# A matmul with batch norm whose instructions a planner orders: the planner's durations replaced by traced ones

## The chip, the cores and the metric

The kernel runs on one core of one Trainium2 chip. The metric is the device time of one execution in microseconds (us), the median of several. The engines are named as in the profile: PE (matrix unit) with PEld (its weight loads), DVE (vector), ACT (scalar), POOL (GpSimd) and SP (which here only issues DMAs).

## The reference

```python
y = np.matmul(x, weight)                      # x 16 x 512 x 1024, weight 1024 x 768, float32
mean = np.mean(y, axis=(0, 1), keepdims=True)
var = np.var(y, axis=(0, 1), keepdims=True)
y_norm = (y - mean) / np.sqrt(var + eps)
return (gamma * y_norm + beta).astype(np.float32)
```

The 16 x 512 rows make 8192. Every output waits for the mean and the variance of its column over all 8192 rows, so no store can start before a column's last product.

## The kernel before

**Tiling.** The rows are 16 chunks `c` of 512 rows (2 MB of x each); the 768 columns are six tiles `nt` of 128. x is loaded as bfloat16 by DMAs that POOL issues (L403, four for a chunk), and turned by DVE transposes (L435, two for a chunk of 512 rows, L428 in chunks 2, 3 and 6) so that the contraction lies on the partitions. Chunk `c` starts at row `m0` = 512 c; below, "the turn of m0=6144" is that of chunk 12.

**Stage 1 (to about 108 us).** While x arrives, column tiles 0 and 1 are computed with rows on the partitions (`rows_unit`, matmuls of L510, two halves of a chunk, 16 matmuls each). Each half is followed by four tasks: ACT squares it into one of three buffers `sq_sb` (L659), DVE adds it to `sum1` (`add_rows`, L662), POOL or DVE adds the squares to `sum2` or `sum3` (`add_squares`, L666), and ACT keeps it as bfloat16 (L672). The gaps of stage 1 are filled with matmuls of column tiles 2 to 5 (L575), ACT copies of some turned chunks (`part_chunk`, L547) and matmuls of L814. Then POOL merges the sums (L795, L800), PE adds them over the partitions (`sums_rows`, L871), and scale and shift follow.

**Stage 2 (to 187 us).** The other column tiles run from the kept x (L575), each followed by statistics (L711) and a copy to bfloat16 (L715, L720). Beside this, finished column tiles are scaled and shifted, brought back to rows by PE transposes (L1044), by DMA transposes (L1106, L1220) or not at all, and stored by DMAs that SP issues (L946, L1085, L1182, L1202).

**Tail (from 187 us).** After the last matmul of column tile 5 (L753) come its statistics, scale and shift, 64 transposes (L1044), ACT copies (L1361) and the last stores (L1364), 4 MB. Two stores of 256 KB held back from column tile 4 (L1255) go ahead of them.

**The planner.** Nothing of this order is written out by hand. Each piece of work is a `Task` with a priority, the engines that can do it, for each of these a pair (time that it occupies the engine, time to its end), and its dependencies and buffers. `arrange` (L122) builds the order when the kernel is built: it takes the engine that can begin something first, among that engine's tasks that can begin within `LOOK` = 0.2 of that moment the one of best priority, and books it. `SEM` is the time between an end and the start that waits for it. `Wires` (L98) books DMAs: one set of wires, serially, with a lead ahead and a tail behind, and eight DMAs under way for a queue. A DVE task with `lock` is not begun while a POOL task is booked, and the other way round. A task with two engines (`add_squares`: POOL or DVE) goes to the one that can begin it first. What `arrange` returns is the order in which each engine executes its instructions; on the chip they then wait for semaphores, and the booked times mean nothing there.

Of the kernel before, what the change touches and what calls it, by code (L numbers as in the profile page):

```python
# [9 lines left out]
class Task:  # L10
# [3 lines left out]
    def __init__(self, prio, engines, emit, deps=(), dma=None, uses=(), takes=()):  # L14
        self.prio, self.engines, self.emit, self.deps = prio, engines, emit, list(deps)
        self.dma, self.uses, self.takes = dma, list(uses), list(takes)
        self.end = self.after = None
        self.hosts = 0
        self.count = 1
        self.lock = False  # L20
        self.slack = self.look = 0.0
        for slot in self.uses + self.takes:
            slot.users.append(self)
# [74 lines left out]
class Wires:  # L98
# [4 lines left out]
    def __init__(self):  # L103
        self.free = 4.3
        self.lanes = {"SP": [], "POOL": [], "ACT": []}
# [16 lines left out]
def arrange(tasks, turns, log=None):  # L122
# [45 lines left out]
    while left:  # L168
# [46 lines left out]
        if t.dma:  # L215
            free[e], t.end = wires.send(e, start, occ, t.dma, t.count)
        t.start, t.engine = start, e
# [10 lines left out]
def kernel(  # L228
# [133 lines left out]
    def dve(occ):  # L362
        return {"DVE": (occ, occ + 0.09)}
# [10 lines left out]
    LINE, PER_KB = 0.00119, 1 / 385.0  # L374
    STORE, XBAR = 1 / 350.0, 1.25

# [71 lines left out]
    for kind, n, *n1 in order:  # L448
# [12 lines left out]
        if m0 == M // 2:  # L461
# [11 lines left out]
        for i in range(rows // QR):  # L473
            c, q = divmod(m0 // QR + i, QPC)
            for j0, j1 in ((0, JW // 2), (JW // 2, JW)) if m0 < CH else ((0, JW),):
                new = q == 0 and j0 == 0
                x_ready[c, q, j1] = task(
                    -1000 + t, dve((2.2 if c in SINGLE else 1.16) * (j1 - j0) / JW + 0.02),
                    turn_x(slot, x_slot[c], m0, i * QR // 32, j0, j1, new), [load],
                    uses=[slot] if new else [slot, x_slot[c]], takes=[x_slot[c]] if new else [])  # L480
                if not new:
                    x_ready[c, q, j1].deps.append(x_ready[c, 0, JW // 2 if m0 < CH else JW])
            x_ready.setdefault((c, q, JW // 2), x_ready[c, q, JW])
        if rows % QR:
            t0 = rows // QR * QR // 32
            m1 = m0 + 32 * t0
            c, q = divmod(m1 // QR, QPC)
            x_ready["tile", m1 // P] = task(
                -1000 + t, dve(0.63), turn_x(slot, x_slot[c], m0, t0, 0, JW, False, P),
                [load, x_ready[c, 0, JW]], uses=[slot, x_slot[c]])  # L490
            x_ready[c, q, JW] = x_ready[c, q, JW // 2] = x_ready["tile", m1 // P]
# [157 lines left out]
    def rows_stats(c, ts, slot, t):  # L649
# [18 lines left out]
        def keep(eng):  # L668
            if "y" not in y_row[c].__dict__:
# [135 lines left out]
    def ga_unit(nt, c, q, cols=QR):  # L805
# [17 lines left out]
        def keep(eng):  # L823
            if "y" not in y_row[c].__dict__:
# [6 lines left out]
        late = 40 if c == C - 1 else -3.0  # L831
        b = task(clock[0] - late, dve(0.609 * cols / CH + 0.05), bn, [t], uses=[slot])
        mine = [h[1] for k, h in ga_half.items() if k[1] == c]
        k = task(clock[0] + 3.4, act(0.48 * cols / CH + 0.03), keep, [b] + mine,
                 uses=[slot] + ([y_row[c]] if mine else []), takes=[] if mine else [y_row[c]])
# [15 lines left out]
    for c in range(RC, C):  # L851
        for q in range(QPC):
            for nt in range(GA):
                ga_unit(nt, c, q)
    merges.append(task(U, dve(0.36), merge(0), [k[1] for k in ends], True))
    merges.append(task(U, pool(0.65), merge(1), [k[2] for k in ends]))
    for h in range(2):
        merges.append(task(U, pool(0.65), more(h), merges[1:]))

# [57 lines left out]
    U = S - 30.0  # L917
    s1 = task(U, pe(0.9), sums_rows, merges, takes=[tot_slot])
    se = task(U, dve(0.8), sums_entry, [s1], True, uses=[tot_slot])
    ag = [task(U, dve(0.25), aggregate_rows(a), [se] + [h[0] for k, h in ga_half.items() if k[0] == a]) for a in range(GA)]  # L920
    rt = task(U, {"ACT": (0.2, 0.3)}, root_rows, ag)
    sc = task(U, dve(0.3), scale_rows, [rt], True)
    sr = task(U + 0.1, dve(0.35), shift_rows, [sc], True)
    p0 = task(U, pe(0.45), spread_rows(0), [sc], takes=[a0_slot])
    p1 = task(U, pe(0.45), spread_rows(1), [sr], takes=[a1_slot])
    p1.look = 0.6
    sh = task(U, act(0.3), shift_sbuf, [p1], uses=[a1_slot])


    def rows_out(c, s0, s1, k):  # L930
# [13 lines left out]
        def store(eng):  # L944
# [4 lines left out]
        keeps = [row_end[k][3] for k in row_end if k[0] == c]  # L949
        a = task(due, dve(0.3 * n), norm, [p0] + keeps, takes=[slot], uses=[y_row[c], a0_slot])  # L950
        b = task(due + 0.4, dve(0.3 * n) if k in ADDED else pool(0.59 * n), add, [a, p1 if k in ADDED else sh],
                 uses=[slot, a1_slot] if k in ADDED else [slot])
        task(due + 1.0, {"SP": (0.38, 0.4)}, store, [b], dma=n * NA * P * 4 / 1024 / 365.0 * 1.024,
             uses=[slot])
# [13 lines left out]
    def finish_tasks(nt):  # L968
# [41 lines left out]
        if nt in ASTAT:  # L1010
            deps = [task(now + 1.0, {"ACT": (1.2, 1.3)}, total, deps)]
        a = task(now + 1.0, dve(0.5), var, deps)
        b = task(now + 1.0, {"ACT": (0.2, 0.3)}, root, [a])
        if nt > GA:
            return task(now + 1.0, dve(0.55), affine, [b], True)
        d = task(now + 1.0, dve(0.1), invert, [b])
# [39 lines left out]
    def ga_block(c, due):  # L1056
# [31 lines left out]
        norms = [task(due, dve(0.25), norm_ga(a), [sr] + [h[1] for k, h in ga_half.items() if k[1] == c], True, uses=[yslot])  # L1088
                 for a in range(GA)]
# [3 lines left out]
        d = task(due, act(0.905), copy, [t], takes=[slot], uses=[bank])  # L1093
        task(due, {"SP": (0.38, 0.4)}, store, [d], dma=RT * NA * P * 4 / 1024 / 365.0 * 1.024, uses=[slot])

# [3 lines left out]
    def raw_turn(nt, c, due):  # L1099
# [3 lines left out]
        def xbar(eng):  # L1103
# [3 lines left out]
            if not gated:  # L1107
# [7 lines left out]

        b = task(due, {"SP": (1.4, 1.4)}, xbar, [col_end[nt, c + i][1] for i in range(GY)] + [gate], dma=XBAR,
                 takes=[slot], uses=[yslot])
        raw[nt, c] = slot, b

# [7 lines left out]
    def raw_spread(nt, fin_task):  # L1127
# [31 lines left out]

        d = task(now, dve(0.35), turn, [fin_task], True)  # L1160
        g = task(now, {"POOL": (0.8, 0.85), "ACT": (0.9, 1.0)}, gather, [d])
        s = task(now, {"POOL": (1.2, 1.25), "ACT": (1.0, 1.1)}, deal, [g])
        t = task(now, act(0.4), keep, [s], takes=[bank])
        raw_aff[nt] = bank, t, s, row[:, 1]

    def raw_block(nt, c, due):
# [17 lines left out]

        a = task(due, dve(1.18), norm_raw, [t, turned], takes=[slot], uses=[bank, rslot])
        on = RAWADD[nt]
# [4 lines left out]
    def col_block(nt, c, due, fin_task, held=False):  # L1191
# [30 lines left out]
        b = task(due + 0.5, {"SP": (1.4, 1.4)}, xbar, [a], dma=XBAR,  # L1222
                 takes=[t_slot] + ([slot] if MODE[nt][c // GY] == "xact" else []), uses=[yslot])
        if MODE[nt][c // GY] == "xpool":
            def store_x(eng):
# [3 lines left out]
        else:  # L1229
# [3 lines left out]

            d = task(due + 1.0, act(0.9), convert, [b], uses=[slot, t_slot])
            d.slack = 1.0
# [32 lines left out]
    for nt in range(GA, NT - 1):  # L1268
        if nt == NT - 2:
            for i, c in enumerate(LATE):  # L1270
                part_chunk(c, clock[0] + 0.0 + 4.0 * i, {"DVE": (0.63, 0.7), "ACT": (1.05, 1.1)},
                           i == 0, 4.0 / 4, [col_end[NT - 3, late[-1]][1]])
# [52 lines left out]

    su = task(E - 5.0, dve(0.5), sum_up, [col_end[nt, c][0] for c in range(C - 2)])
    ag = task(E - 50.0, dve(0.25), aggregate,
# [11 lines left out]
    for c, r0, rows in ends:  # L1339
# [23 lines left out]
        def store(eng, slot=slot, m0=m0, count=count):  # L1363
# [48 lines left out]
```

## Time and profile before

| what | value |
|---|---|
| time, median of 3 runs (lowest, highest) | 205.97 us (205.72, 206.15) |
| profiled execution, first to last instruction (span) | 204.1 us |
| median less span: what lies around the span, if the profiled execution took as long as the median | 1.87 us |
| busy: PE, DVE, ACT, POOL | 189.3, 159.3, 146.2, 124.1 us |
| first matmul of the product, end of the last one | 12.14, 186.6 us |
| HBM read, written | 36.71, 25.17 MB |

The profile keeps one execution. It shows when each instruction began and how long it took, the idle time of an engine and what ended it, and the DMAs; the trace also has the moments at which a DMA's semaphore tells of its landing. A profile of such a kernel is read from PE outwards: first where PE stands still, then how late the data of each of its blocks were ready.

### The profile page before, as it was taken

What the parts mean: (1) busy time and instruction counts of PE and PEld (TensorE: products, weight loads), DVE (VectorE), ACT (ScalarE), POOL (GpSimd) and SP (SyncE); (2) the same over time, 40 slices, a digit from 0 to 9 for tenths busy, and PEclk for the clock granted to TensorE, in tenths of its full rate; (3) what the DMA queues carried; (4) which work ended last, traced back from release to release, by engine and by line L of the source; (5) the groups of instructions that cost most, each with busy time, mean ns of one, the idle gap of its engine ahead of it and who ended that gap; (6) DMA issues with size and microseconds to landing.
All of it is one profiled execution on the core that took longest, in us unless ns stands there. A gap on an engine that the chain in (4) does not pass through costs nothing.

```text
span 204.1 us, 3510 instructions
## 1 busy us (share of the span) xinstructions
PE 189.3 (93%) x1210; PEld 114.5 (56%) x1210; DVE 159.3 (78%) x250; ACT 146.2 (72%) x260; POOL 124.1 (61%) x150
## 2 busy tenths in 40 slices
PE   7969999999999999999999999999999999997900
PEld 3457554657488888777865444444444445544600
DVE  4031879999999999969989998987999878657900
ACT  2001461368989999899978766999998959956950
POOL 7776954877499989997403999389613312940000
PEclk9999999999999999999999999999999999999965
DMA  4999999999999999999686899899999999999998
GB/s 71 172 199 196 176 196 196 196 197 197 190 193 197 197 196 196 196 197 195 103 181 200 297 339 336 248 301 328 295 322 227 336 303 274 347 343 310 310 347 253
DMA packets 98562, 48.74 MB, mean 239 GB/s; under 512 B 24304, under 2 KB 98032, under 8 KB 98544
## 3 DMA queue, kind: packets, MB, share of 16 engines
q0 software_dynamic: 34624, 18.36, 65.5%
q1 hardware_dynamic: 63920, 30.16, 52.6%
q8 instruction: 9, 0.15, 0.3%
q14 instruction: 9, 0.07, 0.1%
HBM read 36.71 MB, written 25.17 MB: 303 GB/s over the span
## 4 chain that ended last, share of the span: by engine, by line
PE 86%; ACT 3%; DMA 3%; POOL 2%; issue 1%; ACTq 0%; DVE 0%; POOLq 0%
PE y_ps L575 54%; PE y_ps L510 24%; PE y_ps L814 4%; ACT o_sb L1361 3%; DMA ring<-in_x_dram 3%; PE o_ps L1044 1%; POOL ring L403 1%; POOL w_sb L387 1%; PE y_ps L753 1%; PE a_ps L903 1%; PE o_ps L1074 0%; ACTq L1407 0%; PE idle_ps L591 0%; PE tot_ps L871 0%; ACT ring L1252 0%
## 5 line engine op out<-in xcount | busy, mean ns | idle before, releaser
L575 PEld LDWEIGHTS <-w_sb 128*128 128x128 bf16 x520 | 50.3, 97 | 57.6
L575 PE MATMUL y_ps<-xT_sb,w_sb 128*128 128x512 bf16 (+1 forms) x272 | 59.3, 371 | 0.0
L575 PE MATMUL y_ps<-x_pl,w_sb 128*128 128x512 bf16 x248 | 57.4, 379 | 0.0
L403 POOL DMA_DIRECT2D ring<-in_x_dram x76 | 47.2, 626 | 14.4 <-DMA ring<-in_x_dram 5.5
L510 PE MATMUL y_ps<-w_sb,xT_sb 128*128 128x256 bf16 x448 | 50.6, 273 | 1.7 <-DMA ring<-in_x_dram 1.6
L510 PEld LDWEIGHTS <-xT_sb 128*128 128x128 bf16 x448 | 43.5, 98 | 9.4 <-DVE xT_sb L435 2.9
L435 DVE STREAM_TRANSPOSE xT_sb<-ring 128x1024 f32<-128x1024 f32 (+1 forms) x29 | 31.2, 1111 | 14.1 <-DMA ring<-in_x_dram 13.9
L711 DVE BATCH_NORM_STATS2 stats<-y_ps 128x6 f32<-128x512 f32 x46 | 30.9, 687 | 7.7 <-PE y_ps L575 7.2
L715 ACT CAST y_sb<-y_ps 128x512 bf16<-128x512 f32 x51 | 29.0, 593 | 10.4 <-DVE stats L711 6.3
L547 ACT COPY x_pl<-xT_sb 128x1024 bf16<-128x1024 bf16 x32 | 32.8, 1063 | 1.7 <-DVE xT_sb L435 1.7
L942 POOL TENSOR_TENSOR ring<-ring,sum 128x1024 f32<-128x1024 f32 (+1 forms) x11 | 23.8, 2188 | 14.9 <-ACT y_ps L724 10.9
L659 ACT ACTIVATE sq_sb<-y_ps 128x512 f32<-128x512 f32 x28 | 16.3, 610 | 16.2 <-PE y_ps L510 15.9
L666 POOL TENSOR_TENSOR sum<-sum,sq_sb 128x512 f32<-128x512 f32 x20 | 25.6, 1278 | 3.0 <-ACT sq_sb L659 1.7
L662 DVE TENSOR_TENSOR sum<-y_ps,sum 128x512 f32<-128x512 f32 x28 | 18.9, 675 | 6.3 <-ACT sq_sb L659 5.3
L672 ACT CAST y_sb<-y_ps 128x512 bf16<-128x512 f32 x28 | 16.3, 594 | 8.2 <-DVE sum L662 8.0
L1178 POOL TENSOR_TENSOR ring<-ring,sum 128x1024 f32<-128x1024 f32 x6 | 14.8, 2477 | 9.8 <-issue 8.5
L937 DVE TENSOR_TENSOR ring<-y_sb,a_ps 128x1024 f32<-128x1024 bf16 (+1 forms) x16 | 16.7, 1079 | 0.1
L1044 PE MATMUL o_ps<-ident,y_sb 128*128 128x128 bf16 x104 | 13.1, 221 | 1.6 <-DVE y_sb L1348 1.5
L1232 ACT CAST ring<-ring 128x1024 f32<-128x1024 bf16 x13 | 13.8, 1063 | 0.6 <-DMA ring<-y_sb 0.6
L1145 POOL COPY sum<-sum 32x256 f32<-32x256 f32 (+1 forms) x17 | 5.8, 340 | 13.4 <-DVE sum L1142 6.5
L428 DVE STREAM_TRANSPOSE xT_sb<-ring 128x2048 bf16<-128x2048 bf16 x6 | 13.5, 2290 | 0.1
L591 PE MATMUL idle_ps<-idle_sb 128*128 128x512 f32 x18 | 9.6, 688 | 1.5 <-DVE idle_sb L316 1.5
(104 smaller groups left out, 153.7 us busy)
## 6 DMA issues: line engine op xcount, KB each, us to landing
out_dram<-ring SPq DMA_DIRECT2D x37, 512.0 KB, 3.4
ring<-in_x_dram POOLq DMA_DIRECT2D x52, 256.0 KB, 8.8
out_dram<-o_sb SPq DMA_DIRECT2D x6, 512.0 KB, 4.7
ring<-in_x_dram POOLq DMA_DIRECT2D x16, 128.0 KB, 5.9
w_sb<-in_weight_dram POOLq DMA_DIRECT2D x8, 192.0 KB, 6.2
out_dram<-ring SPq DMA_DIRECT2D x6, 256.0 KB, 3.0
ring<-in_x_dram POOLq DMA_DIRECT2D x4, 192.0 KB, 7.8
out_dram<-o_sb SPq DMA_DIRECT2D x3, 256.0 KB, 2.5
```

The costliest lines, as they stand in the source:

```text
L403: bi = seq(nc.gpsimd.dma_start(x_bf[32 * i:32 * i + 32], src[:, :, KQ * i:KQ * (i + 1)]))
L435: seq(nc.vector.transpose(dst, src[:, :, jw0:jw1]))
L510: seq(nc.tensor.matmul(y_ps[:, s], x_of(c, jw, e, t * P, (t + 1) * P), w_sb[:, jw, e, 0:NA], start=(s == 0 and jw == 0 and e == 0), stop=( ...
L547: seq(nc.scalar.copy(dst, pairs) if eng == "ACT" else ENG[eng].tensor_copy(dst, pairs))
L575: seq(nc.tensor.matmul(y_ps, w_sb[:, jw, e, nt * P:(nt + 1) * P], moving(c, jw, e, q0 * QR, q1 * QR, parted), start=(jw == 0 and e == 0 an ...
L659: seq(nc.scalar.activation(sq_sb[:, 0:n], slot.tile[:, 0:n], AF.Square))
L662: seq(nc.vector.tensor_add(sum1, slot.tile[:, 0:n], sum1))
L666: seq(ENG[eng].tensor_add(acc, acc, state["sq"][:, 0:n]))
L711: seq(nc.vector.bn_stats(dst, slot.tile))
L715: seq(nc.scalar.copy(y(nt, c), slot.tile))
L937: seq(nc.vector.tensor_mul(slot.o, y_row[c].y[:, s0:s1], aff[0][:, None, :].to_broadcast([P, n, NA])))
L942: seq(ENG[eng].tensor_add(slot.o, slot.o, row[:, None, :].to_broadcast([P, n, NA])))
```

## The change

Only what `arrange` reckons with is changed. No task, dependency, buffer or priority is added or taken away, and no instruction is changed; the order in which the engines execute them follows from the new numbers. The numbers of the lines rise by 1 behind L21, by 7 in all behind L113, by 8 behind L1117 and by 9 behind L1223.

```diff
-        self.free = 4.3
+        self.free = 4.21
-    def send(self, queue, t, hold, took, count):
-        soft = queue == "POOL"
+    def send(self, queue, t, hold, took, count, turned=False):
+        if turned:
+            t = max(t, self.ready(queue))
+            self.free = max(self.free, t + 0.722) + took
+            land = max(self.free + 0.375, t + hold + 1.4)
+            self.lanes[queue].append(land)
+            return max(t + hold, land - 2.325), land
+        first, last = (1.095, 1.0425) if queue == "POOL" else (0.722, 0.441)
         for _ in range(count):
             t = max(t, self.ready(queue)) + hold / count
-            self.free = max(self.free, t + (1.0 if soft else 0.5)) + took / count
-            land = self.free + (1.3 if soft else 0.6)
+            self.free = max(self.free, t + first) + took / count
+            land = self.free + last
...
-    SEM, LOOK = 0.06, 0.2
+    SEM, LOOK = 0.03, 0.2
...
-    STORE, XBAR = 1 / 350.0, 1.25
+    STORE, XBAR, TURN = 1 / 345.85, 1.12, {"SP": (1.143, 1.143)}
...
-            t, {"POOL": (2.68 * rows / CH + 0.535 * also, 2.68 * rows / CH + 0.535 * also)}, load_x(m0, rows, slot, between),
+            t, {"POOL": (2.57 * rows / CH + 0.6 * also,) * 2}, load_x(m0, rows, slot, between),
...
-                    -1000 + t, dve((2.2 if c in SINGLE else 1.16) * (j1 - j0) / JW + 0.02),
+                    -1000 + t, dve((2.2 if c in SINGLE else 1.15) * (j1 - j0) / JW + 0.01),
...
-        s = task((now + 4.2 if c < RC - 2 else 0), {"POOL": (1.36, 1.36 + 0.05), "DVE": (0.62, 0.7)}, add_squares, [a],
+        s = task((now + 4.2 if c < RC - 2 else 0), {"POOL": (1.22, 1.276), "DVE": (0.60, 0.682)}, add_squares, [a],
...
-            part_chunk(c, clock[0] + (4.0 if c < EARLY else 20.0), act(1.05))
+            part_chunk(c, clock[0] + (4.0 if c < EARLY else 20.0), {"ACT": (0.946, 1.056)})
...
-    merges.append(task(U, dve(0.36), merge(0), [k[1] for k in ends], True))
-    merges.append(task(U, pool(0.65), merge(1), [k[2] for k in ends]))
+    merges.append(task(U, {"DVE": (0.489, 0.567)}, merge(0), [k[1] for k in ends], True))
+    merges.append(task(U, {"POOL": (0.70, 0.737)}, merge(1), [k[2] for k in ends]))
...
-        b = task(due + 0.5, {"SP": (1.4, 1.4)}, xbar, [a], dma=XBAR,
+        b = task(due + 0.5, TURN, xbar, [a], dma=XBAR,
+        b.turned = True
...
-        task(due + 0.6 * (n - 1), {"SP": (0.6, 0.6)}, store, [d], dma=count * P * P * 4 / 1024 * STORE * 1.024,
+        task(due + 0.6 * (n - 1), {"SP": (0.4, 0.4)}, store, [d], dma=count * P * P * 4 / 1024 * STORE * 1.024,
```

Some twenty more pairs are changed in the same way by 0.01 to 0.4 us (statistics of the two last chunks, scale and shift, the stores of column tiles 0 and 1, the spreading of a column's scale over rows). `add_rows` keeps its 0.608, L711 its 0.609, L659 its 0.494.

More of the change, by code (lines that the diff above doesn't have):

```diff
@@ L215, in arrange @@
         if t.dma:
-            free[e], t.end = wires.send(e, start, occ, t.dma, t.count)
+            free[e], t.end = wires.send(e, start, occ, t.dma, t.count, t.turned)
         t.start, t.engine = start, e
@@ L831, in ga_unit @@
         late = 40 if c == C - 1 else -3.0
-        b = task(clock[0] - late, dve(0.609 * cols / CH + 0.05), bn, [t], uses=[slot])
+        b = task(clock[0] - late, {"DVE": (0.342, 0.42)}, bn, [t], uses=[slot])
         mine = [h[1] for k, h in ga_half.items() if k[1] == c]
-        k = task(clock[0] + 3.4, act(0.48 * cols / CH + 0.03), keep, [b] + mine,
+        k = task(clock[0] + 3.4, {"ACT": (0.29, 0.375)}, keep, [b] + mine,
                  uses=[slot] + ([y_row[c]] if mine else []), takes=[] if mine else [y_row[c]])
@@ L917 @@
     U = S - 30.0
-    s1 = task(U, pe(0.9), sums_rows, merges, takes=[tot_slot])
-    se = task(U, dve(0.8), sums_entry, [s1], True, uses=[tot_slot])
-    ag = [task(U, dve(0.25), aggregate_rows(a), [se] + [h[0] for k, h in ga_half.items() if k[0] == a]) for a in range(GA)]
+    s1 = task(U, pe(0.81), sums_rows, merges, takes=[tot_slot])
+    se = task(U, {"DVE": (0.63, 0.707)}, sums_entry, [s1], True, uses=[tot_slot])
+    ag = [task(U, {"DVE": (0.25, 0.28)}, aggregate_rows(a), [se] + [h[0] for k, h in ga_half.items() if k[0] == a]) for a in range(GA)]
     rt = task(U, {"ACT": (0.2, 0.3)}, root_rows, ag)
[L922 to L925, printed above, removed]
+    sc = task(U, {"DVE": (0.27, 0.361)}, scale_rows, [rt], True)
+    sr = task(U + 0.1, {"DVE": (0.27, 0.357)}, shift_rows, [sc], True)
+    p0 = task(U, pe(0.48), spread_rows(0), [sc], takes=[a0_slot])
+    p1 = task(U, pe(0.48), spread_rows(1), [sr], takes=[a1_slot])
     p1.look = 0.6
-    sh = task(U, act(0.3), shift_sbuf, [p1], uses=[a1_slot])
+    sh = task(U, {"ACT": (0.28, 0.37)}, shift_sbuf, [p1], uses=[a1_slot])
     def rows_out(c, s0, s1, k):
@@ L1010, in finish_tasks @@
         if nt in ASTAT:
-            deps = [task(now + 1.0, {"ACT": (1.2, 1.3)}, total, deps)]
+            deps = [task(now + 1.0, {"ACT": (0.82, 0.91)}, total, deps)]
         a = task(now + 1.0, dve(0.5), var, deps)
@@ L1014, in finish_tasks @@
         if nt > GA:
-            return task(now + 1.0, dve(0.55), affine, [b], True)
+            return task(now + 1.0, {"DVE": (0.78, 0.87)}, affine, [b], True)
         d = task(now + 1.0, dve(0.1), invert, [b])
@@ L1114, in xbar @@
             seq(bi)
[L1116 removed]
+        b = task(due, TURN, xbar, [col_end[nt, c + i][1] for i in range(GY)] + [gate], dma=XBAR,
                  takes=[slot], uses=[yslot])
+        b.turned = True
         raw[nt, c] = slot, b
@@ L1158, in keep @@
             seq(nc.scalar.copy(a_ps[:, 0:2 * P], row.rearrange("p i n -> p (i n)")))
[L1160 to L1163, printed above, removed]
+        d = task(now, {"DVE": (0.467, 0.543)}, turn, [fin_task], True)
+        g = task(now, {"POOL": (0.98, 1.036), "ACT": (0.91, 1.02)}, gather, [d])
+        s = task(now, {"POOL": (1.43, 1.48), "ACT": (1.15, 1.25)}, deal, [g])
+        t = task(now, {"ACT": (0.302, 0.38)}, keep, [s], takes=[bank])
         raw_aff[nt] = bank, t, s, row[:, 1]
@@ L1183, in store @@
                 out_flat[m0:m0 + n * P, nt * P:(nt + 1) * P].rearrange("(s p) n -> p s n", p=P), slot.o))
-        a = task(due, dve(1.18), norm_raw, [t, turned], takes=[slot], uses=[bank, rslot])
+        a = task(due, {"DVE": (1.13, 1.218)}, norm_raw, [t, turned], takes=[slot], uses=[bank, rslot])
         on = RAWADD[nt]
@@ L1270 @@
             for i, c in enumerate(LATE):
-                part_chunk(c, clock[0] + 0.0 + 4.0 * i, {"DVE": (0.63, 0.7), "ACT": (1.05, 1.1)},
+                part_chunk(c, clock[0] + 0.0 + 4.0 * i, {"DVE": (0.58, 0.67), "ACT": (0.946, 1.056)},
                            i == 0, 4.0 / 4, [col_end[NT - 3, late[-1]][1]])
@@ L1324, in affine @@
         seq(nc.vector.scalar_tensor_tensor(fss, coef, rstd, base, op0=ALU.mult, op1=ALU.add))
-    su = task(E - 5.0, dve(0.5), sum_up, [col_end[nt, c][0] for c in range(C - 2)])
+    su = task(E - 5.0, {"DVE": (0.72, 0.808)}, sum_up, [col_end[nt, c][0] for c in range(C - 2)])
     ag = task(E - 50.0, dve(0.25), aggregate,
```

18 lines of the change are left out of this document (10 added, 8 removed).

## The prediction

> **What bounds the kernel now.** I read the page first, then the windows, the chain of waits, the time lines of DVE and POOL about 80 us, and SP's at the end. The page and the windows:
>
> ```profile
> PE 189.3 (93%) x1210; PEld 114.5 (56%) x1210; DVE 159.3 (78%) x250; ACT 146.2 (72%) x260; POOL 124.1 (61%) x150
> ...
> PE 86%; ACT 3%; DMA 3%; POOL 2%; issue 1%; ACTq 0%; DVE 0%; POOLq 0%
> ...
> 72.00:97.00 25.00, 25.00 (x204) 19.60 (x202) 22.55 (x28) 24.07 (x38) 22.44 (x28) 1.00 1.45 196
> 97.00:108.00 11.00, 11.00 (x94) 8.72 (x93) 9.86 (x28) 9.18 (x28) 2.45 (x6) 1.00 0.76 151
> ```
>
> The first pair of the windows' columns is the length and PE's busy time: from its first product at 12.14 to the last at 186.6 PE stands still for some 0.15 us in all, at clock 1.00. So nothing in the middle can be won. The time is the head (12.14), PE's fixed work (174.5) and the tail (17.5); a new order adds whatever PE is made to wait, and changes the tail.
>
> The tail, from SP's time line (start, length, line, operation, count):
>
> ```profile
> 183.56 1.41 SPq L1182 DMA_DIRECT2D out_dram<-ring  x1
> 187.53 1.20 SPq L1255 DMA_DIRECT2D out_dram<-ring  x2
> 189.31 10.56 SPq L1364 DMA_DIRECT2D out_dram<-o_sb  x11
> ```
>
> By the trace's landing events the store of 183.56 lands at 189.53, and from there the landings follow each other by 0.76 us for 256 KB and 1.51 for 512 KB up to 203.15: the DMAs are the bound of the tail, with a little work still queued when it begins. A store on idle DMAs lands 2.78 after its issue (120.58 to 123.36), that is 1.27 and its 1.51; 1.40 by a 256 KB one (109.10 to 111.25). With nothing queued at 187.5 the two held stores and the four small ones behind them would land at 189.55, 190.31, 190.97, 191.44, 192.32 and 193.08 instead of 190.29 to 193.33. An order that empties the queue is worth 0.25 us (0.13 by the other lead), and no more: **0.2**. Likewise a tail that begins later hides only these 0.2.
>
> **What the change moves.** I compared the built instructions of both kernels, engine by engine. PE's order is the same, except that 32 transposes of L1044 stand four matmuls later at about 170 us, the same number behind the same line: 0. The head's order is the same: 0. On DVE, ACT, POOL and SP tasks change places from 24 us on. Each costs nothing unless PE gets its data or its bank later than it asks for them, so I looked for the blocks of PE with least to spare: those of the last chunks in stage 1, whose turn waits for loads that the DMAs bring at 196 GB/s without a pause (the last column of the windows).
>
> DVE's time line there:
>
> ```profile
> 75.62 2.25 DVE L662 TENSOR_TENSOR sum<-y_ps,sum 128x512 f32<-128x512 f32 x3
> 77.78 0.90 DVE L666 TENSOR_TENSOR sum<-sum,sq_sb 128x512 f32<-128x512 f32 x1
> 78.87 2.37 DVE L435 STREAM_TRANSPOSE xT_sb<-ring 128x1024 f32<-128x1024 f32 x2 [0.20 <-DMA ring<-in_x_dram]
> 81.17 2.25 DVE L662 TENSOR_TENSOR sum<-y_ps,sum 128x512 f32<-128x512 f32 x3
> 83.33 0.68 DVE L666 TENSOR_TENSOR sum<-sum,sq_sb 128x512 f32<-128x512 f32 x1
> 84.02 2.37 DVE L435 STREAM_TRANSPOSE xT_sb<-ring 128x1024 f32<-128x1024 f32 x2
> 86.32 1.45 DVE L662 TENSOR_TENSOR sum<-y_ps,sum 128x512 f32<-128x512 f32 x2
> 89.37 2.37 DVE L435 STREAM_TRANSPOSE xT_sb<-ring 128x1024 f32<-128x1024 f32 x2 [1.60 <-DMA ring<-in_x_dram]
> 91.66 1.02 DVE L666 TENSOR_TENSOR sum<-sum,sq_sb 128x512 f32<-128x512 f32 x1
> ```
>
> The pairs of L435 turn chunks 11, 12 and 13. The first half of chunk 12's pair ends at 85.26 (84.02 and 1.24), and PE takes it at 85.41: 0.15 to spare. Chunk 13 has 0.45 (90.61, 91.06), `sums_rows` 0.1 (99.33, 99.43). Chunks 9 and 10 have 2 or more.
>
> And POOL's:
>
> ```profile
> 68.08 3.84 POOL L403 DMA_DIRECT2D ring<-in_x_dram  x6
> ...
> 74.13 4.00 POOL L666 TENSOR_TENSOR sum<-sum,sq_sb 128x512 f32<-128x512 f32 x3
> 78.06 2.56 POOL L403 DMA_DIRECT2D ring<-in_x_dram  x4
> 80.64 2.64 POOL L666 TENSOR_TENSOR sum<-sum,sq_sb 128x512 f32<-128x512 f32 x2
> 83.22 2.57 POOL L403 DMA_DIRECT2D ring<-in_x_dram  x4
> ```
>
> **Two L666 at once exclude each other.** The DVE one of 77.78 lasts 0.90 and that of 91.66 lasts 1.02, where one alone lasts 0.68. POOL's end at 78.13 (74.13 and 4.00) and 92.13 (90.84 and 1.29); both DVE ones end 0.55 after that. L662, which reads one operand from PSUM, is not held up by them (three in 2.25 at 81.17, as at 75.62, with POOL in L666 from 82.00). The planner knows this rule (`lock`), and keeps them apart by its bookings; on the chip whichever comes first wins. So the question is how well the new numbers place them. The change sets POOL's L666 to 1.22 from 1.36. In the trace three of them take 3.93 to the next instruction (74.13 to 78.06) and two 2.58, so 1.3 each; and `add_rows` is booked at 0.608, where three in a row take 2.25.
>
> The order between chunk 11's turn and chunk 12's, before: DVE L662 three times, L666; after: L662 twice, L666, L662, L666. On POOL, from the load issues of 68.08 on, before: eight L403, three L666, four L403, two L666; after: four L403, two L666, four L403, three L666, four L403, one L666.
>
> POOL after: 68.08 and 2.56 for four issues: 70.64; two L666, 2.58: 73.22; four issues, 2.58: 75.80; three L666, 3.93: 79.73; four issues: 82.31; so its next L666 runs from **82.31 to 83.59**. The loads don't suffer: the issues that move by 2.6 us have 9 and more us to their landing.
>
> DVE after: chunk 11's turn waits for its load as before, and ends at 81.24; two L662, 1.45 from 81.17: 82.62; the next begins 0.08 earlier, as L666 does at 83.33, so at **82.54**. POOL has had the memory since 82.31. DVE's L666 then ends at 83.59 and 0.55: 84.14. L662 from 84.06, the second L666 from 84.66 (0.60 apart, 83.33 less 82.72), the turn from 85.26, its first half ends 1.24 later at 86.50, and PE begins 0.03 behind it: 86.53, where it began at 85.41. **PE waits 1.12.** The Trainium skill (SBUF — State Buffer, section "SBUF: two separate sides") calls this an exclusive lock, in which the later one fully blocks; by that the L666 would take its whole 0.68 behind POOL, and the wait be 1.25. The rows' 0.55 decides.
>
> The other places: a pair collides in the same way at 72.5 ahead of chunk 10's turn; that moves by 0.3, and PE has 2 to spare: 0. Ahead of chunk 13's turn one more L666 of DVE waits for a square (L659) of chunk 12. PE comes to chunk 13 1.12 later itself, at 92.18, and the 0.68 fit in unless the square is over 1 us later than now: 0, at most 0.3. `sums_rows` needs the last L666, merged by L795 and L800 on POOL; all of it follows PE by the same amount: 0, at most 0.2. From 108 to 186 us, PE's banks are free 2 us and more before it asks, the x copies (L547) 5 us; moves of 1 to 2 us there cost 0, at most 0.3. The tail: PE ends 1.12 later, past the queue's end; what was queued no longer matters, which is the 0.2.
>
> **The sum.** 204.1 + 1.12 - 0.2 = 205.0 for the span. The median lies 1.87 above the span of the profiled execution: **206.9 us**, 0.45% more.
>
> **The rivals.** Measurements of this kernel tell about 0.2% (0.4 us) from no change.
>
> 1. *DVE comes first at the port.* It decides at 0.23 us: were POOL's L666 that much later, or DVE's that much earlier, DVE would hold it. For: the 0.23 is what is left of six additions. Against: no row has POOL slower than 1.36 in a row. Price: DVE's L666 from 82.54, L662 83.14, L666 83.74, turn 84.34, half done 85.58; PE waits 0.2. At chunk 13 its L666 goes ahead of the turn, 0.6 against 0.45 and these 0.2; with POOL now late and ACT behind it, 0 to 0.4. In sum 0.2 to 0.6, less 0.2: 206.0 to 206.4, not slower by what can be told.
> 2. *The change does nothing to the time*: the new places find enough room everywhere, and the tail's queue is empty sooner. For: PE now stands still nowhere, with 0.15 here and 0.1 there to spare. Against: the L666 more ahead of chunk 12's turn. 0 to -0.25: 205.7 to 206.0.
> 3. *More than one stall*: the bounds above at once, or a DMA queue that is longer at the tail because POOL's adds (L1178, now three in a row) come later. 0.8 more at most: 207.3 to 207.8.
>
> **The numbers.** Forecast (206.6 to 207.3) 0.60; rival 1 0.22, of it 0.04 over 0.2%; rival 2 0.11, of it 0.05 under -0.2% by what the runs scatter; rival 3 0.07. Slower 0.60 + 0.07 + 0.04 = 0.71; faster 0.05; same 0.24. The range from 205.9 to 207.5 leaves out most of rival 2 and half of rival 3, and holds the low bound of the wait.
>
> **What would show it.** In the profile after, L666 on DVE near 82.5 with 1.5 us instead of 0.68, beside an L666 of POOL; the turn of chunk 12 at 85.2; a wait of PE (L510) for DVE's L435 of about 1.1 in the list of waits, which has none now; PE's last product at 187.7. If that L666 lasts 0.68 and POOL's is the longer one, rival 1 holds; if PE waits nowhere, rival 2. The forecast is wrong if PE waits elsewhere for 0.5 us or more, or if the last stores don't follow PE's end.

## The result, and the profile after

The changed kernel takes **207.25 us** (median of 6 runs, 207.06 to 207.67), the kernel before 206.06 (6 runs as well): ratio 1.0066, 95% interval 1.005 to 1.0081. The ratio is not the quotient of these two medians, which is 1.0058 (1.19 us). The profiled execution took 207.51, its span 205.7 (before 204.1).

In the changed kernel the line numbers are higher by 7 (L435 is L442, L662 is L669, L666 is L673, L659 is L666, L672 is L679, L814 is L821, L871 is L878) or by 8 and 9 in the late part.

The page after; its second line is the shares of the chain of work that ended last:

```profile
PE 190.2 (92%) x1196; PEld 114.7 (56%) x1210; DVE 159.8 (78%) x251; ACT 145.1 (71%) x262; POOL 122.9 (60%) x147
...
PE 44%; DMA 20%; ACT 15%; DVE 7%; issue 5%; POOL 4%; ACTq 1%; DVEq 0%; POOLq 0%
```

No engine has much more work than before: PE's 0.9 us lie ahead of its first product (busy 9.90 us to 12.14, before 9.07). But the chain, of which PE had 86%, now leaves PE and goes through DMA, ACT and DVE: PE is made to wait. Its list of waits (us in total, times, longest) has, beside the wait for the first load, which was there before, two rows in stage 1 that are new:

```profile
PE y_ps L517 <- DMA ring<-in_x_dram: 0.9, 1, 0.9
PE y_ps L517 <- DVE xT_sb L442: 0.5, 2, 0.3
PE y_ps L821 <- ACT y_sb L679: 0.2, 1, 0.2
```

Of the 0.5 us for L442, 0.3 lie at 26 us and only 0.2 at chunk 12. At chunk 14 two things end nearly together: the first half of the turn at 97.93, and at 97.97 ACT's copy L679, which the row names. These waits sum to less than the loss, since a wait is only shown where it stands out between two instructions. A better measure is how much later PE begins the same block. PE's order is nearly the same (4 of its 1210 weight loads differ, in e1, e2, e3 and e7 8 to 28), so each weight load can be laid beside its twin in the trace of before. The table does this at six places, for the profiled execution of every kernel of this study (us later than before), with the length of the tail (from the issue of the first held store, L1255, to the landing of the last store: 15.62 before) and the ratio of the times with its interval.

| kernel | first product, 12.11 | chunk 11, 80.17 | chunk 12, 85.41 | chunk 13, 91.06 | chunk 14, 96.71 | L575 at 173.52 | tail | ratio |
|---|---|---|---|---|---|---|---|---|
| after | 0.12 | 0.27 | 0.71 | 1.02 | 1.36 | 1.69 | 15.61 | 1.0066 (1.005, 1.0081) |
| e4 one add later | -0.12 | 0.08 | 0.44 | 2.77 | 3.12 | 3.45 | 15.61 | 1.0172 (1.014, 1.0205) |
| e6 POOL's add later | 0.22 | 0.39 | 0.48 | 1.15 | 1.16 | 1.15 | 15.62 | 1.0023 (1.0011, 1.0035) |
| e9 ACT's sums later | -0.13 | -0.02 | 0.43 | 0.74 | 0.74 | 0.74 | 15.60 | 1.0045 (1.0029, 1.006) |
| e10 all moves | -0.06 | -0.07 | 0.02 | 0.02 | 1.99 | 1.98 | 15.61 | 1.0170 (1.0134, 1.0206) |
| e11 e6 and e9 | -0.24 | -0.07 | 0.16 | 0.52 | 0.52 | 0.52 | 15.61 | 1.0038 (1.0025, 1.0051) |
| e15 three places | -0.04 | -0.07 | 0.16 | 0.16 | 0.49 | 0.50 | 15.59 | 1.0025 (1.0011, 1.004) |
| e16 e4, four buffers | 0.83 | 0.80 | 1.27 | 2.07 | 2.42 | 2.81 | 18.17 | 1.0210 (1.0192, 1.0229) |
| e17 e10, four buffers | 0.24 | -0.05 | 0.04 | 0.04 | 0.04 | 0.10 | 18.16 | 1.0159 (1.0137, 1.018) |
| e1 stage 1 numbers | 1.23 | 1.55 | 2.50 | 2.50 | 2.70 | 3.92 | 17.83 | 1.0235 (1.021, 1.026) |
| e2 other numbers | -0.02 | 0.38 | 0.47 | 0.47 | 0.47 | 0.41 | 16.42 | 1.0049 (1.002, 1.0079) |
| e3 SEM 0.06 | 0.28 | 0.44 | 0.44 | 0.44 | 1.27 | 1.20 | 16.28 | 1.0115 (1.0085, 1.0145) |
| e7 spacing | 0.41 | 0.10 | 0.28 | 0.75 | 1.00 | 2.64 | 15.70 | 1.0104 (1.0087, 1.0122) |

Two rows need a note. In e1 four products stand ahead of transposes at 173.52, so its value there is taken at the last product. In e7 two products stand ahead of the blocks of chunks 11 and 12, so its entries there compare unlike matmuls; what shows at chunk 13 is lost at chunk 12.

The first column differs although the order is the same in all of them to 20 us: it is the scatter of one execution, and the second column holds it too. The ten kernels of the table that have the order of after to 80 us stand between -0.07 and 1.55 there. In the row of after, 0.27 is there by chunk 11; **1.42 more come between 80 and 173 us**, all of them by 100: 0.44 at chunk 12, 0.31 at chunk 13, 0.34 at chunk 14, 0.24 where `sums_rows` (L878) begins and 0.09 within it. The tail is as long as before. The measured 0.66% is 1.36 us. So the loss is made in 20 us at the end of stage 1.

DVE's time line there (start, length, line, count):

```profile
82.54 0.68 DVE L673 TENSOR_TENSOR sum<-sum,sq_sb 128x512 f32<-128x512 f32 x1
83.14 0.68 DVE L669 TENSOR_TENSOR sum<-y_ps,sum 128x512 f32<-128x512 f32 x1
83.74 1.16 DVE L673 TENSOR_TENSOR sum<-sum,sq_sb 128x512 f32<-128x512 f32 x1
84.82 2.35 DVE L442 STREAM_TRANSPOSE xT_sb<-ring 128x1024 f32<-128x1024 f32 x2
...
90.17 0.69 DVE L673 TENSOR_TENSOR sum<-sum,sq_sb 128x512 f32<-128x512 f32 x1 [1.62 <-ACT sq_sb L666]
90.78 2.36 DVE L442 STREAM_TRANSPOSE xT_sb<-ring 128x1024 f32<-128x1024 f32 x2
...
95.48 0.69 DVE L673 TENSOR_TENSOR sum<-sum,sq_sb 128x512 f32<-128x512 f32 x1 [0.97 <-ACT sq_sb L666]
...
96.69 2.36 DVE L442 STREAM_TRANSPOSE xT_sb<-ring 128x1024 f32<-128x1024 f32 x2
```

The three pairs of L442 turn chunks 12, 13 and 14; ahead of each stands an addition of squares. They begin at 84.82, 90.78 and 96.69, where before they began at 84.02, 89.37 and 95.20. The additions ahead of chunks 13 and 14 wait for ACT's squares, and DVE's queue waits with them. POOL's line beside the first:

```profile
79.96 2.57 POOL L410 DMA_DIRECT2D ring<-in_x_dram  x4
82.54 1.80 POOL L673 TENSOR_TENSOR sum<-sum,sq_sb 128x512 f32<-128x512 f32 x1
```

POOL's L673 lasts 1.80, where one alone lasts 1.29. Both began at 82.54; DVE's took its usual 0.68, so DVE came first. At 83.74 the next one of DVE found POOL at it until 84.34, and ended 0.56 behind that. The planner had booked POOL's from 81.29 to 82.51 and DVE's from 82.51: in its plan they don't touch, on the chip POOL is 1.25 late.

ACT's line, with the squares of chunks 12 and 13 (L666):

```profile
89.39 0.74 ACT L666 ACTIVATE sq_sb<-y_ps 128x512 f32<-128x512 f32 x1
90.95 0.60 ACT L666 ACTIVATE sq_sb<-y_ps 128x512 f32<-128x512 f32 x1 [0.82 <-DVE sum L673]
...
94.28 0.60 ACT L727 ACTIVATE y_sb<-y_ps 128x512 bf16<-128x512 f32 x1
...
94.86 0.59 ACT L666 ACTIVATE sq_sb<-y_ps 128x512 f32<-128x512 f32 x1
...
96.28 0.62 ACT L731 ACTIVATE y_ps<-y_ps 128x512 f32<-128x512 f32 x1
...
96.88 0.62 ACT L666 ACTIVATE sq_sb<-y_ps 128x512 f32<-128x512 f32 x1
```

The second square waits for DVE's addition of the first: in the program as it is built, both use the same one of the three buffers. L727 and L731 are the two sums of column tile 2 that stand ahead of the squares of chunk 13.

### The profile page after: what moved, and what is told of

Its sections match the earlier page's. It is cut to its first block, busy times and chain, and to the rows that moved or that the text cites. A ratio compares the mean times of both kernels' runs of the same rounds, so it can differ in the third digit from the quotient of the medians.

```text
span 205.7 us, 3500 instructions
## 1 busy us (share of the span) xinstructions
PE 190.2 (92%) x1196; PEld 114.7 (56%) x1210; DVE 159.8 (78%) x251; ACT 145.1 (71%) x262; POOL 122.9 (60%) x147
## 4 chain that ended last, share of the span: by engine, by line
PE 44%; DMA 20%; ACT 15%; DVE 7%; issue 5%; POOL 4%; ACTq 1%; DVEq 0%; POOLq 0%
PE y_ps L582 34%; DMA ring<-in_x_dram 12%; DMA w_sb<-in_weight_dram 6%; ACT x_pl L554 4%; PE y_ps L821 4%; ACT o_sb L1370 3%; POOL ring L410 3%; ACT sq_sb L666 3%; PE y_ps L517 3%; ACT y_sb L679 2%; DMA ring<-y_sb 2%; PE o_ps L1051 2%; DVE xT_sb L442 1%; DVE x_pl L554 1%; DVE xT_sb L435 1%
## 5 line engine op out<-in xcount | busy, mean ns | idle before, releaser
L582 PE MATMUL y_ps<-xT_sb,w_sb 128*128 128x512 bf16 (+1 forms) x264 | 58.6, 371 | 0.4
L582 PE MATMUL y_ps<-x_pl,w_sb 128*128 128x512 bf16 x242 | 56.6, 379 | 0.3
L442 DVE STREAM_TRANSPOSE xT_sb<-ring 128x1024 f32<-128x1024 f32 (+1 forms) x29 | 31.1, 1109 | 12.6 <-DMA ring<-in_x_dram 12.6
L722 ACT CAST y_sb<-y_ps 128x512 bf16<-128x512 f32 x51 | 28.8, 587 | 13.6 <-DVE stats L718 6.1
L554 ACT COPY x_pl<-xT_sb 128x1024 bf16<-128x1024 bf16 x31 | 31.8, 1069 | 1.7 <-DVE xT_sb L442 1.7
L666 ACT ACTIVATE sq_sb<-y_ps 128x512 f32<-128x512 f32 x28 | 17.0, 626 | 19.0 <-PE y_ps L517 17.2
L673 POOL TENSOR_TENSOR sum<-sum,sq_sb 128x512 f32<-128x512 f32 x20 | 26.1, 1303 | 4.4 <-ACT sq_sb L666 3.8
L1186 POOL TENSOR_TENSOR ring<-ring,sum 128x1024 f32<-128x1024 f32 x6 | 14.3, 2412 | 17.1 <-DVE ring L1182 17.1
L669 DVE TENSOR_TENSOR sum<-y_ps,sum 128x512 f32<-128x512 f32 x28 | 18.9, 674 | 5.9 <-ACT sq_sb L666 4.7
L679 ACT CAST y_sb<-y_ps 128x512 bf16<-128x512 f32 x28 | 15.9, 618 | 2.5 <-DVE sum L669 2.5
L435 DVE STREAM_TRANSPOSE xT_sb<-ring 128x2048 bf16<-128x2048 bf16 x6 | 13.5, 2289 | 0.2 <-DMA ring<-in_x_dram 0.2
L1241 ACT CAST ring<-ring 128x1024 f32<-128x1024 bf16 x13 | 13.3, 1048 | 0.5 <-DMA ring<-y_sb 0.4
L598 PE MATMUL idle_ps<-idle_sb 128*128 128x512 f32 x18 | 10.5, 739 | 1.5 <-DVE idle_sb L323 1.5
L1153 POOL COPY sum<-sum 32x64 f32<-32x64 f32 (+1 forms) x14 | 4.6, 326 | 10.6 <-DVE sum L1150 10.0
```

The source lines that it names most:

```text
L442: seq(nc.vector.transpose(dst, src[:, :, jw0:jw1]))
L554: seq(nc.scalar.copy(dst, pairs) if eng == "ACT" else ENG[eng].tensor_copy(dst, pairs))
L582: seq(nc.tensor.matmul(y_ps, w_sb[:, jw, e, nt * P:(nt + 1) * P], moving(c, jw, e, q0 * QR, q1 * QR, parted), start=(jw == 0 and e == 0 an ...
L666: seq(nc.scalar.activation(sq_sb[:, 0:n], slot.tile[:, 0:n], AF.Square))
L669: seq(nc.vector.tensor_add(sum1, slot.tile[:, 0:n], sum1))
L673: seq(ENG[eng].tensor_add(acc, acc, state["sq"][:, 0:n]))
```

## The experiments

Three theories. **A**, the forecast's: the additions ahead of chunk 12's turn and their collision are the loss. **B**: the last limit wins; ACT's order in these 20 us, through the squares that DVE's additions wait for, sets the turns of chunks 13 and 14 and the merge of the sums. **C**: the loss comes from the late part, the stores and the model of transfers.

In the edits `pick` finds a task by name, engine and booked start (not the start in the trace), and `behind` moves it behind another in the finished order.

**e4: one addition moved behind the turn.**

```diff
     order = arrange(tasks, turns)
+    behind(pick("add_squares", "DVE", 83.72), pick("emit", "DVE", 85.60))
```

> The kernel after, with one DVE add_squares (chunk 10, second half, 83.74 in the trace of after) moved from ahead of the turn of chunk 12 to behind it; nothing else. Both theories: the turn begins at 83.8 instead of 84.82, its first half is done at 85.0, and PE's wait of 0.18 at chunk 12 goes. Theory A (the forecast's: the additions ahead of the turn of chunk 12, with the collision, are the loss): PE keeps 0.4 to 0.5 of it to the end, 206.8. Theory B (the last limit wins: ACT works without a pause from 84 to 101, its order sets the turns of chunks 13 and 14 and the merge of the sums, whatever PE lost before): PE only waits longer at chunk 13, the first product of L821 stays at 98.0 and the time at 207.2 (207.1 to 207.4). Theory C (the late part and the stores are the loss): 207.2 as well, told from B by the next runs.

209.45 us (208.26 to 210.54): all three theories were wrong. Chunk 12 lost only 0.36 (0.44 less 0.08), but chunk 13 lost 2.33. In this execution POOL's addition came first (82.18; DVE's from 82.61 lasted 1.42), so the turn of chunk 12 began at 84.55 and not at 83.8. ACT's line in e4 shows why chunk 13 is late:

```profile
85.57 0.59 ACT L679 CAST y_sb<-y_ps 128x512 bf16<-128x512 f32 x1
87.94 0.60 ACT L666 ACTIVATE sq_sb<-y_ps 128x512 f32<-128x512 f32 x1 [1.78 <-DVE sum L673]
```

The moved addition ended at 87.82 (86.83 and 0.99), and the square began behind it. Squares have three buffers, and the addition that empties one had been put off. A new candidate: additions of squares stand between two limits, **ahead of a turn they hold up PE's data, behind it they hold a buffer that ACT needs**.

**e6: POOL's addition of 82.54 moved behind its load issues.**

```diff
+    behind(pick("add_squares", "POOL", 81.29), pick("emit", "POOL", 82.51))
```

> The kernel after, with POOL's add_squares of 82.54 (1.80 long) moved behind the four load issues that follow it; nothing else. So no addition of POOL stands beside DVE's two. If the collision makes the difference: DVE's second add_squares lasts 0.68 instead of 1.16, the turn of chunk 12 begins at 84.34 instead of 84.82 and PE's wait of 0.18 there goes. If the length is due to something else it stays 1.16. In time: theory A 206.8 to 207.0, theories B and C 207.2.

206.31 us, about two thirds of the loss gone (1.0066 to 1.0023, and the intervals don't overlap); more than any of the theories allows. The profiled execution is the slowest of its nine (207.01), so its row in the table shows more loss than the median has. DVE's line:

```profile
82.79 0.68 DVE L673 TENSOR_TENSOR sum<-sum,sq_sb 128x512 f32<-128x512 f32 x1
83.39 0.68 DVE L669 TENSOR_TENSOR sum<-y_ps,sum 128x512 f32<-128x512 f32 x1
83.99 0.68 DVE L673 TENSOR_TENSOR sum<-sum,sq_sb 128x512 f32<-128x512 f32 x1
84.59 2.36 DVE L442 STREAM_TRANSPOSE xT_sb<-ring 128x1024 f32<-128x1024 f32 x2
```

Without POOL beside it the second addition lasts 0.68, not 1.16: the 0.48 are the collision. A second gain was not foreseen: ACT's two squares of chunk 12 follow each other at 89.53, where after had a wait of 0.82 between them for DVE's addition of 90.17. So DVE's addition ahead of the turn of chunk 14 waits 0.21 for ACT, where after's waits 0.97. The reason is in the built program: the moved task also changed which buffer each square gets, and the second square of chunk 12 no longer has that of the first (so too in e11, e15 and e17; in e4, e9, e10 and e16 it has). This run therefore changed two things, and its gain is not the collision's alone.

**e9: two tasks of ACT later.**

```diff
+    behind(pick("square_sum", "ACT", 94.52), pick("keep", "ACT", 95.61))
+    behind(pick("keep_sum", "ACT", 92.49), pick("keep", "ACT", 95.61))
```

> The kernel after, with two tasks of ACT (L727 at 94.28 and L731 at 96.28, sums of column tile 2, chunk 4) moved behind ACT's square and copy of chunk 13 (97.35); nothing else. Theory B: the square of 94.86 begins at 94.3, DVE's add_squares that waits for it 0.6 earlier, so the turn of chunk 14 at 96.1 instead of 96.69 and L821 on PE at 97.4 instead of 98.0; the last square 1.2 earlier, so the merge of sums no longer holds L878; in all 0.9 less, 206.35 (206.1 to 206.6). Theory A: it was no part of the loss, 207.0 to 207.3. Theory C: 207.2.

206.85 us, 1.0045: a third of the loss, half of what B expected, by ratios whose intervals overlap. The trace is clearer: the loss at chunk 14 and behind it is gone (0.74 at chunk 13 and to the end), as B said; those at chunks 12 and 13 stay.

**e10: all of these places on DVE and ACT.** The two edits above (e4's and e9's), and

```diff
+    behind(pick("add_squares", "DVE", 89.21), pick("emit", "DVE", 91.09))
```

> The kernel after, with four tasks moved: one DVE add_squares behind the turn of chunk 12, one DVE add_squares (90.17) behind the turn of chunk 13, and ACT's L727 and L731 behind the square and copy of chunk 13. Theory B: with no addition ahead of the turns and ACT's squares in time PE waits nowhere from 80 to 102; 206.0 to 206.2, the time of before. Theory A: the waits at chunks 12 and 13 go, those behind stay in part: 206.4 to 206.7. Theory C: 207.2, since nothing behind 108 is changed.

209.69 us (207.81 to 210.47), although chunks 12 and 13 are on time (0.02). ACT waits 0.86 and 1.39 for the moved additions, and chunk 14 comes 1.99 late. Again the buffers. The profiled execution is the fastest of the six (207.81); what makes the others up to 2.7 us longer is in no trace.

**e1 and e2: the numbers halved.** e1 takes only the new numbers of stage 1 into the kernel before, e2 only the others.

```diff
 e1
+    SEM, LOOK = 0.03, 0.2
+    t, {"POOL": (2.57 * rows / CH + 0.6 * also,) * 2}, load_x(m0, rows, slot, between),
+    {"POOL": (1.22, 1.276), "DVE": (0.60, 0.682)}, add_squares
...
 e2
+    first, last = (1.095, 1.0425) if queue == "POOL" else (0.722, 0.441)
+    STORE, XBAR, TURN = 1 / 345.85, 1.12, {"SP": (1.143, 1.143)}
...
```

> The kernel before with only those new numbers that the planner uses in stage 1 (SEM, the load issue, the turns, add_squares, the copies of turned chunks, the statistics and merges at its end); the model of DMAs and all other numbers are the old ones. PE's order is that of both kernels, and on every engine the order to 103 us is that of after. Theory A/B (the loss is made in stage 1, by the additions ahead of the turns, their collisions and ACT's order): the same waits as in after at 86, 92, 98 and 101, and the whole loss, 206.9 to 207.4. Theory C (late part, stores and transfers): 205.7 to 206.2.

> The other half: the kernel before with only the new model of DMAs, the new transfer times and the new numbers of the work behind 103 us. On every engine the order to 103 us is that of before; PE's differs behind 107 by where some transposes are hosted. Theory A/B: PE waits nowhere from 12 to 187, 205.6 to 206.1. Theory C: the loss, 206.8 to 207.3.

e1 takes 210.43 (its profiled execution, 211.97, is the slowest of six), e2 206.82 (205.45 to 208.3). In sum stage 1 went as A and B said: PE loses 1.41 from chunk 11 to 99.5 us in e1 (1.55 to 2.96; 1.33 in after), and nothing from chunk 11 to chunk 14 in e2 beyond 0.09. But the places differ: e1 loses 0.95 at chunk 12, nothing at chunk 13, 0.20 at chunk 14 and 0.26 at the sums. With the same order as after, POOL's addition came first here (83.64; DVE's from 84.08 lasted 1.40). The times did not go as said: e1 loses about 1 us more by the last product (2.96 to 3.92; 0.71 of it L1044 waiting for DVE's L1026 at 174.8) and 2.2 in the tail, e2 0.8 in the tail. In both the stores queue up: e2's last store ahead of the tail lands at 190.74, 2.8 us behind the issue of the first held one (before 2.0, after 0.8), and the rest follow at 1.51 for 512 KB. So C is wrong for after, whose tail is 15.61, but the late numbers are not harmless: whether the stores are done when PE ends depends on both halves together.

**e3: SEM alone undone.**

```diff
-    SEM, LOOK = 0.03, 0.2
+    SEM, LOOK = 0.06, 0.2
```

> The kernel after with one number undone: the planner's SEM back from 0.03 to 0.06. With it the order has no DVE add_squares between the turn of chunk 11 and that of chunk 12, nor ahead of that of chunk 13 (one stands ahead of chunk 11's and one ahead of chunk 14's). Theory A/B: no wait of PE at chunks 12 and 13, most of the loss is gone, 205.9 to 206.4. Theory C: 207.0 to 207.4, since the DMA model is the new one.

208.39 us. Chunks 12 and 13 lose nothing (0.44 at 80, 85 and 91), as expected of an order without additions ahead of their turns. But the turn of chunk 14 is late by 0.83, and the tail is 0.66 longer. The same 0.03 that took away one wait moved tasks 5 and 100 us further on.

**e11: e6 and e9 together.**

> The kernel after with the two moves that helped alone: POOL's add_squares of 82.54 behind the load issues, and ACT's L727 and L731 (94.28, 96.28) behind the square and copy of chunk 13. Alone they brought the ratio to before from 1.0066 to 1.0023 and to 1.0045. If their gains add: about 1.000, 205.6 to 205.9. If both act on the same limit (the turn of chunk 14 and the merge of sums): no better than the better one, 206.1 to 206.4.

206.56 us, 1.0038 (1.0025 to 1.0051): the gains don't add, and by the intervals it can't be told from e6 alone. Chunk 12 loses 0.23, chunk 13 0.36, and nothing behind it:

```profile
89.66 0.69 DVE L673 TENSOR_TENSOR sum<-sum,sq_sb 128x512 f32<-128x512 f32 x1 [1.66 <-ACT sq_sb L666]
90.27 2.37 DVE L442 STREAM_TRANSPOSE xT_sb<-ring 128x1024 f32<-128x1024 f32 x2
```

What is left is the addition ahead of the turn of chunk 13, which waits for ACT.

**e15: that one moved too** (e11, and the edit of e10).

> The kernel after with the two moves of the last run but one (POOL's addition behind its load issues, ACT's L727 and L731 later; 206.56) and the DVE addition of 89.7 behind the turn of chunk 13, three buffers. There the turn of chunk 13 began at 90.27 behind that addition, which waited for ACT; PE came 0.36 late. If this is what is left: the turn begins at 89.4, PE has no wait, 205.8 to 206.2. If the moved addition again holds a buffer from ACT (it did where it alone stood late): 207 and more.

206.37 us, 1.0025. Chunk 13 is on time (0.16), but chunk 14 loses 0.33: the moved addition now stands at 92.11 beside one of POOL (91.46 to 92.75) and lasts 1.20. The collision has only gone to another place.

**e16 and e17: four buffers for squares**, in e4 and in e10. The planner still books three; the order on every engine stays.

```diff
-    sqpool = ctx.enter_context(tc.tile_pool(name="sqpool", bufs=SQ))
+    sqpool = ctx.enter_context(tc.tile_pool(name="sqpool", bufs=SQ + 1))
-    PAD = 50
+    PAD = 0
```

> The kernel of the one moved addition (209.45) with four buffers for squares instead of three (the planner still books three, the order of every engine is the same; 1.2 KB of padding are given up for it). There ACT waited 1.78 for DVE's late addition ahead of a square of chunk 11 and 0.82 ahead of one of chunk 12, and PE 2.2 at chunk 13. If the moved addition cost so much because it held a buffer of the three: these waits go, and with the wait at chunk 12 gone too the time is under that of after, 206.5 to 207.1. If it cost so much for another reason: 208.5 and more.

> The kernel with all four moved tasks (209.69) with four buffers for squares. If the three limits are the additions ahead of the turns, the buffers and ACT's order, none is left: PE waits nowhere from 80 to 102, 205.7 to 206.2, the time of before. If something else of stage 1 or the late part holds after back: 206.6 and more.

In e16 ACT's wait of 1.78 is gone, and chunk 13 loses 0.80 instead of 2.33; ACT's wait of 0.82 for DVE's addition stays, since that square has the buffer of the one before it here too, with four. In e17 none of stage 1's waits is left:

```profile
85.45 3.66 PE L517 MATMUL y_ps<-w_sb,xT_sb 128*128 128x256 bf16 x32
...
91.10 3.66 PE L517 MATMUL y_ps<-w_sb,xT_sb 128*128 128x256 bf16 x32
...
96.75 2.88 PE L821 MATMUL y_ps<-xT_sb,w_sb 128*128 128x256 bf16 x24
99.48 0.95 PE L878 MATMUL tot_ps<-ones,tot 128*128 128x1 f32 x8
```

These are the times of before to 0.05 (85.41, 91.06, 96.71, 99.43), with all the other new numbers and the late order of after in place. So in this execution additions ahead of the turns, the buffers that they hold and ACT's order are the whole loss of after in stage 1, and its late part adds 0.06. The times (210.37 and 209.34) are still long. The tails of 18.17 and 18.16, told below, are 2.55 of it. The profiled execution of e17 is the fastest of its four (208.48), and where the others lose 0.7 to 1.0 us more is in no trace.

**e7: numbers nearer to rows in a row.**

```diff
-    {"POOL": (1.22, 1.276), "DVE": (0.60, 0.682)}, add_squares
+    {"POOL": (1.33, 1.380), "DVE": (0.60, 0.682)}, add_squares
-    dve(0.608), add_rows
+    dve(0.70), add_rows
```

> The kernel after with two numbers nearer to what rows in a row take: add_squares on POOL 1.33 instead of 1.22 (three take 3.93), add_rows 0.70 instead of 0.608 (three take 2.24). The order has two DVE additions of squares ahead of the turn of chunk 12, none ahead of that of chunk 13. If the loss comes from numbers that are too short where additions follow each other, PE's waits at chunks 12 to 14 go: 205.8 to 206.3. If any new set of numbers only throws the order about, the time can be anything from 206 to 209.

207.99 us: not better. Chunks 12 and 14 lose 0.47 and 0.25, and the sums 1.2 where L878 waits for POOL's merge. Truer numbers gave another order, and this one has other places without room.

No version beats the kernel before. e17 with the tail of the others would have its last landing at 203.23 (187.62, where its first held store is issued, and 15.61), where before has 203.15: an estimate from its fastest execution, the time of before. It was not run.

## Why the prediction was right, and where not

The forecast was 206.9 with a range to 207.5; measured 207.25, a ratio of 1.0066 where 1.0045 was forecast. The stage and the kind of the loss were right: additions and a collision that hold up DVE's turns. The terms were not: the wait at chunk 12 was 0.44 and not 1.12, and 0.98 came at three places that the sum puts at 0. By the forecast's own sign (L666 on DVE lasts 0.68 and POOL's is the longer one) it was the first rival that took place, with a time above its 206.0 to 206.4. That the total came so near is in good part luck.

- *The order and the moment.* DVE's L666 was forecast for 82.54 and began at 82.54. Reading the new order on the old rows was good to 0.01 on DVE, and to 0.23 on POOL (82.31 forecast, 82.54 measured). POOL's steps were right as well (14.24 us for 14.23); its load issues began at 68.30 and not at 68.08.
- *Who comes first.* The first rival decided "at 0.23 us", and it was 0.23: DVE held the memory, as the rival says. But the rival went on with L666 of 0.60 at 83.74, and there POOL was still at it. So the turn came at 84.82, between the rival's 84.34 and the forecast's 85.26, and PE lost 0.44 instead of 1.12 or 0.2. The step that failed is "POOL has had the memory since 82.31"; neither case saw that the one put off collides with the next. It was not the mechanism that failed: where POOL did come first, in e1, the collision went as forecast, and PE lost 0.95 at chunk 12. But the loss to the end of the sums was 1.49 there and 1.42 in after, so who comes first moves the loss and hardly changes it. The Trainium skill (SBUF — State Buffer, section "Who interferes with whom") says that the order of issue, not the shape of the work, decides who blocks. The rows agree: 1.80 on POOL where DVE is first, 1.16 on DVE where POOL is.
- *Chunk 13.* "0, at most 0.3" because PE comes late itself: measured 0.31. The addition waited for a square, as named. That PE would come 1.12 late itself was not so (0.71 in all), and ACT's next square waited for the addition in turn.
- *Behind it.* L814 was not reckoned with: 0.34. `sums_rows` "at most 0.2": 0.33. It waits for DVE's merge L802, which lasts 0.93 beside POOL's L807 (0.57 in before), and then for the last L807. Both losses come through ACT's late squares. Either remedy takes both away: the two sums of column tile 2 moved out of the way (e9), or another buffer for the second square of chunk 12 (e6). I had looked at DVE's and POOL's order for what moved ahead of a turn, and not at ACT's for what moved ahead of the squares that these wait for. These 0.67 are more than what is missing in the forecast.
- *108 to 186 us: 0.* Right: 1.69 late at 100 and at 173.
- *The tail, -0.2.* Wrong: 15.62 before and 15.61 after. The queue was emptied as hoped, and the two held stores landed 2.37 and 3.09 behind the first issue (before 2.75 and 3.51). But the third store from `o_sb`, 256 KB, is issued 2.76 behind it in both and landed at 5.03 (before 5.05): it took 2.28, where the forecast reckons with 1.27 and 0.76, and it landed 0.94 behind the store ahead of it (before 0.77), so it was no longer the queue that held it. From there the landings follow each other as before, so an emptied queue gave nothing.
- *Sum:* 0.44 + 0.31 + 0.34 + 0.24 + 0.09 = 1.42 instead of 1.12 - 0.2 = 0.92; 1.36 by the ratio.

## What to carry to other kernels

An order that a planner finds from booked durations is right only as far as the bookings hold: POOL's additions in a row were booked at 1.22 and take 1.31 (three from 76.04 to 79.96), by 82 us the plan was 1.25 us ahead of POOL, and a collision that the plan's `lock` had avoided took place on the chip. Where PE never waits, a new set of numbers, truer or not, has little to win: all five sets tried here (after, e1, e2, e3, e7) lost. In after the loss began at the blocks with less than 0.5 us to spare: look there at every engine whose result the block waits for through another (here ACT, two steps away). Moving a task that holds up a block is no repair by itself; ask first what it releases, and whether the built program still gives each tile the same buffer.

## What the runs showed of the hardware

**Stores from a shifted tile were slower.** In e16 and e17 the 512 KB stores from `o_sb` land 1.86 us apart, those from `ring` 1.51 as in all other kernels. The page's row of DMA issues (KB each, us from issue to landing), in after and in e17:

```profile
out_dram<-o_sb SPq DMA_DIRECT2D x6, 512.0 KB, 4.7
```

```profile
out_dram<-o_sb SPq DMA_DIRECT2D x6, 512.0 KB, 6.3
```

The padding that was given up moved `o_sb` from addresses that are multiples of 256 bytes to 64 bytes past one; the pieces are 512 bytes. The tails of these two kernels are 2.55 us longer than the others' usual 15.61. The tile `ring` did not move. The Trainium skill (DMA: Bandwidth & Descriptors, section "How a descriptor splits into AXI transactions") says that when a descriptor does not start at a multiple of 256 bytes, its first transaction starts at the boundary below, and the bytes ahead of the start are fetched, unused, and cost beats of 32 bytes. By that 18 beats take the place of 16 for such a piece, an estimate from the page of 1.70 us; the 1.86 agree in direction, and the measurement decides the size. No other offset was tried, so that the offset is the cause is supported and not shown.

**Near ties.** Seven kernels have the same order on DVE and POOL up to these two additions. In the profiled executions of e1, e4 and e16 POOL's came first and DVE's lasted 1.40 to 1.53; in those of after, e9, e10 and e17 DVE's came first and POOL's lasted 1.78 to 1.80. From e16, a line of each engine:

```profile
83.33 1.53 DVE L673 TENSOR_TENSOR sum<-sum,sq_sb 128x512 f32<-128x512 f32 x1
```

```profile
83.02 1.28 POOL L673 TENSOR_TENSOR sum<-sum,sq_sb 128x512 f32<-128x512 f32 x1
```

So the order that is built does not settle a near tie. e4 and e10 differ between executions by 2.3 and 2.7 us, the kernel before by 1.0 in 14. That the tie is the cause of this was not tested, and it can't be the only one: e2, which has the order of before in stage 1, differs by 2.85 in 12.
